# Whole-row loads and another release for the first store in a rotary-embedding kernel

## The chip, the cores and the metric

The kernel runs on one core of one Trainium2 chip. The metric is the device time of one execution in microseconds (us), lower is better. The profile is one execution recorded by the hardware profiler; its span is the time between the first and the last recorded event, a little less than the execution's own time.

## The reference

Rotary position embedding with interleaved pairs. `x` has the shape (8, 2048, 16, 64) in float32, `cos` and `sin` have (2048, 32). All inputs are random normal.

```python
x_pairs = x.reshape(batch, seq_len, num_heads, head_dim // 2, 2)
x1 = x_pairs[..., 0]
x2 = x_pairs[..., 1]
cos = cos[None, :, None, :].copy()
sin = sin[None, :, None, :].copy()
out1 = x1 * cos - x2 * sin
out2 = x1 * sin + x2 * cos
out = np.stack([out1, out2], axis=-1).reshape(batch, seq_len, num_heads, head_dim)
```

67.1 MB of float32 come in and as many go out.

## The kernel before

The text calls one batch entry a row: there are eight, and one holds 2048 positions of 1024 values. The positions are spread over the 128 partitions, 16 consecutive ones (K) on each, so a row is 16384 values per partition. In SBUF the rows stand in bfloat16, in one buffer `rows_sb` with five slots (NX); row b stands in slot b modulo 5. A load from GpSimd's DMA queue turns float32 into bfloat16 on the way, and a store turns it back. A row is 8.4 MB in HBM and 4.2 MB in SBUF.

`rotate` (line 65) works on a row in place with three VectorE operations. The first writes row times sine table into the scratch tile `qt` (line 79), the second multiplies the row by the cosine table (line 80), and the third adds `qt` to the row with the neighbours of each pair exchanged (line 85). The sine table holds the sine with alternating sign, and both tables are repeated over the 16 heads by a stride of zero.

Everything is issued in the order written out by hand, and an instruction waits only for what it needs. The dependencies are tracked per region of a tile. GpSimd issues all DMAs but two; the first four sixteenths of row 0 (the tile `st`) come by SyncE's queue in float32 and are turned to bfloat16 by ScalarE (line 99), and the last four sixteenths of row 7 leave the same way at the end (lines 131 and 132). In GpSimd's order:

- the rest of row 0, `cos`, `sin`, then rows 1 and 2 as one DMA (line 56), row 3 (line 54), and row 4 in two DMAs, its first fourteen sixteenths and then its last two (REST);
- the store of rows 0 and 1 as one DMA (line 63), then the store of row 2 (line 61);
- the load of rows 5 and 6 as one DMA into slots 0 and 1, once those have been stored, and the load of row 7 into slot 2, once that has been stored;
- the store of rows 3 and 4, that of rows 5 and 6, and that of the first twelve sixteenths of row 7.

VectorE builds the tables from `sin` and `cos` (lines 101 to 103), rotates row 0 in two pieces and then the rows 1 to 7.

The store of rows 0 and 1 is held back on purpose by two tiny copies on ScalarE:

```python
nc.scalar.copy(out=mark, in_=rows_sb[:1, 4, K - REST - 1, :1])
nc.scalar.copy(out=rows_sb[:1, 0, 0, :1], in_=rows_sb[:1, 0, 0, :1])
store(0, 2)
```

The first reads one value of row 4 that arrives with its first DMA, the second copies a value of row 0 onto itself. ScalarE goes in order, so the second copy comes after the first, and the store, which reads row 0, comes after both. Near the end, line 130 holds the tail back in the same manner: it writes a value into slot 1 and so waits until row 6 has been stored.

Of the kernel before, what the change touches and what calls it, by code (L numbers as in the profile page):

```python
# [2 lines left out]

# [4 lines left out]


@with_exitstack  # L10
def kernel(
    ctx: ExitStack,
    tc: tile.TileContext,
    x: bass.AP,
    cos: bass.AP,
    sin: bass.AP,
    out: bass.AP,
):
    nc = tc.nc
    fp32 = mybir.dt.float32  # L20
    bf16 = mybir.dt.bfloat16
    mult = mybir.AluOpType.mult
    add = mybir.AluOpType.add

    B, S, H, D = x.shape
    P = 128
    K = S // P
    D2 = D // 2
    HD = H * D
    NX = 5  # L30
    HEAD = 4
    TAIL = 4
    REST = 2

    x_t = x.rearrange("b (p k) h d -> p b k (h d)", p=P, k=K)
    out_t = out.rearrange("b (p k) h d -> p b k (h d)", p=P, k=K)
    cos_t = cos.rearrange("(p k) c -> p (k c)", p=P, k=K)
    sin_t = sin.rearrange("(p k) c -> p (k c)", p=P, k=K)

    consts = ctx.enter_context(tc.tile_pool(name="consts", bufs=1))  # L40
    stage = ctx.enter_context(tc.tile_pool(name="stage", bufs=1))

    cos_sb = consts.tile([P, K * D2], fp32)
    sin_sb = consts.tile([P, K * D2], fp32)
    c_tab = consts.tile([P, K, D], bf16)
    s_tab = consts.tile([P, K, D], bf16)
    mark = consts.tile([1, 1], bf16)

    rows_sb = consts.tile([P, NX, K, HD], bf16)

    def load(b, n=1, k0=0, k1=K):
        s = b % NX
        if n == 1:
            nc.gpsimd.dma_start(out=rows_sb[:, s, k0:k1], in_=x_t[:, b, k0:k1])  # L54
        else:
            nc.gpsimd.dma_start(out=rows_sb[:, s : s + n], in_=x_t[:, b : b + n])  # L56

    def store(b, n=1, k1=K):
        s = b % NX
        if n == 1:  # L60
            nc.gpsimd.dma_start(out=out_t[:, b, :k1], in_=rows_sb[:, s, :k1])  # L61
        else:
            nc.gpsimd.dma_start(out=out_t[:, b : b + n], in_=rows_sb[:, s : s + n])  # L63

    def rotate(b, k0=0, k1=K):

        nk = k1 - k0
        xp = rows_sb[:, b % NX, k0:k1]
        qt = stage.tile([P, K, HD], bf16, name="qt", tag="work")

        def rows(a):
            return a.rearrange("p k (h e) -> p k h e", h=H, e=D)

        def tab(a):
            return dataclasses.replace(
                a, offset=a.offset + k0 * D, ap=[a.ap[0], [D, nk], [0, H], [1, D]]
            )

        nc.vector.tensor_tensor(out=rows(qt[:, :nk]), in0=rows(xp), in1=tab(s_tab), op=mult)  # L79
        nc.vector.tensor_tensor(out=rows(xp), in0=rows(xp), in1=tab(c_tab), op=mult)  # L80
        q_swap = dataclasses.replace(
            qt, offset=qt.offset + 1, ap=[qt.ap[0], [2, nk * HD // 2], [-1, 2]]
        )
        x3 = xp.rearrange("p k (a j) -> p (k a) j", j=2)
        nc.vector.tensor_tensor(out=x3, in0=x3, in1=q_swap, op=add)  # L85
        return qt

    with tc.manual_schedule():
        head = stage.tile([P, HEAD, HD], fp32, name="st", tag="work")
        nc.sync.dma_start(out=head, in_=x_t[:, 0, :HEAD])  # L90
        load(0, k0=HEAD)
        nc.gpsimd.dma_start(out=cos_sb, in_=cos_t)  # L92
        nc.gpsimd.dma_start(out=sin_sb, in_=sin_t)  # L93
        load(1, 2)
        load(3)
        load(4, k1=K - REST)
        load(4, k0=K - REST)

        nc.scalar.copy(out=rows_sb[:, 0, :HEAD], in_=head)  # L99
        s2 = s_tab.rearrange("p k (i j) -> p (k i) j", j=2)  # L100
        nc.vector.tensor_copy(out=s2[:, :, 0], in_=sin_sb)  # L101
        nc.vector.tensor_scalar_mul(s2[:, :, 1], sin_sb, -1.0)  # L102
        nc.vector.tensor_copy(  # L103
            out=c_tab.rearrange("p k (i j) -> p (k i) j", j=2),
            in_=cos_sb.to_broadcast([P, K * D2, 2]),
        )
        rotate(0, 0, HEAD)
        rotate(0, HEAD, K)
        rotate(1)

        nc.scalar.copy(out=mark, in_=rows_sb[:1, 4, K - REST - 1, :1])  # L111
        nc.scalar.copy(out=rows_sb[:1, 0, 0, :1], in_=rows_sb[:1, 0, 0, :1])  # L112
        store(0, 2)
        rotate(2)
        store(2)
        load(5, 2)
        load(7)
        rotate(3)
        rotate(4)
        store(3, 2)  # L120
        rotate(5)
        rotate(6)
        store(5, 2)
        rotate(7)
        store(7, k1=K - TAIL)


        tail = stage.tile([P, TAIL, HD], fp32, name="st", tag="work")
        last = rows_sb[:, 7 % NX]
        nc.scalar.copy(out=rows_sb[:1, 6 % NX, 0, :1], in_=last[:1, K - 1, :1])  # L130
        nc.scalar.copy(out=tail, in_=last[:, K - TAIL :])  # L131
        nc.sync.dma_start(out=out_t[:, B - 1, K - TAIL :], in_=tail)


# [1 line left out]
_INS = ['x', 'cos', 'sin']  # L136
_OUTS = [((8, 2048, 16, 64), 'float32')]


# [23 lines left out]
```

## Time and profile before

| | before |
|---|---|
| time, median of 3 runs | 316.4 us (316.12 to 316.79) |
| the profiled execution's own time | 316.12 us |
| its span | 314.4 us |
| busy VectorE (DVE) | 210.3 us, 67% of the span |
| busy ScalarE (ACT), GpSimd (POOL) | 8.9 us each |
| read from HBM, written to HBM | 67.63 MB, 67.11 MB |
| one VectorE operation on a whole row | 8.69 us |
| VectorE idle ahead of line 79, waiting for loads | 41.2 us, two times |

In the profile, L79 is line 79 of the kernel; an arrow `out<-in` names the tile that is written and the tiles that are read. The names POOLq and SPq stand for the instruction streams of GpSimd and SyncE that issue DMAs, and the DMA share is the mean busy share of the core's 16 DMA engines. It counts packets by the stretch in which they start, so it can be above 1 in a short one. The GB/s count the bytes at the destination: a load counts its bfloat16 bytes, a store its float32 bytes. "To landing" is the time from the issue of a DMA until all of it has arrived.

### The profile page before, as it was taken

What the parts mean: (1) busy time and instruction counts of PE and PEld (TensorE: products, weight loads), DVE (VectorE), ACT (ScalarE), POOL (GpSimd) and SP (SyncE); (2) the same over time, 40 slices, a digit from 0 to 9 for tenths busy, and PEclk for the clock granted to TensorE, in tenths of its full rate; (3) what the DMA queues carried; (4) which work ended last, traced back from release to release, by engine and by line L of the source; (5) the groups of instructions that cost most, each with busy time, mean ns of one, the idle gap of its engine ahead of it and who ended that gap; (6) DMA issues with size and microseconds to landing.
All of it is one profiled execution on the core that took longest, in us unless ns stands there. A gap on an engine that the chain in (4) does not pass through costs nothing.

```text
span 314.4 us, 118 instructions
## 1 busy us (share of the span) xinstructions
DVE 210.3 (67%) x30; ACT 8.9 (3%) x6; POOL 8.9 (3%) x18
## 2 busy tenths in 40 slices
DVE  0009995099999999999992000899999999910000
ACT  1030000000000000000000000000000000000400
POOL 5000000000000000000000000000000000000000
DMA  8999999999999999999999999999999999999997
GB/s 257 260 284 200 200 204 263 200 200 217 225 233 259 400 534 400 400 434 500 400 200 225 242 200 200 229 238 334 400 484 450 400 400 525 409 400 400 434 434 334
DMA packets 2816, 102.24 MB, mean 325 GB/s; under 512 B 256, under 2 KB 256, under 8 KB 512
## 3 DMA queue, kind: packets, MB, share of 16 engines
q0 software_dynamic: 2528, 98.04, 96.8%
q1 hardware_dynamic: 288, 4.19, 3.4%
HBM read 67.63 MB, written 67.11 MB: 429 GB/s over the span
## 4 chain that ended last, share of the span: by engine, by line
DVE 42%; issue 17%; DMA 14%; another core or an unknown queue 13%; ACTq 1%; POOL 0%; ACT 0%; DVEq 0%; POOLq 0%
DMA out_dram<-rows_sb 14%; DVE rows_sb L80 14%; DVE rows_sb L85 14%; DVE qt L79 14%; ACTq L158 1%; POOL out_dram L63 0%; DVE c_tab L103 0%; ACT rows_sb L130 0%; ACTq L130 0%; DVEq L80 0%; DVEq L79 0%; POOLq L63 0%; POOLq L61 0%
## 5 line engine op out<-in xcount | busy, mean ns | idle before, releaser
L79 DVE TENSOR_TENSOR qt<-rows_sb,s_tab 128x16384 bf16<-128x16384 bf16 (+2 forms) x9 | 69.7, 7743 | 41.4 <-DMA rows_sb<-in_x_dram 41.2
L80 DVE TENSOR_TENSOR rows_sb<-rows_sb,c_tab 128x16384 bf16<-128x16384 bf16 (+2 forms) x9 | 69.7, 7743 | 0.4
L85 DVE TENSOR_TENSOR rows_sb<-rows_sb,qt 128x16384 bf16<-128x16384 bf16 (+2 forms) x9 | 69.7, 7744 | 0.3
L101 DVE CAST s_tab<-sin_sb 128x512 bf16<-128x512 f32 x1 | 0.5, 453 | 23.8 <-DMA sin_sb<-in_sin_dram 23.8
L63 POOL DMA_DIRECT2D out_dram<-rows_sb x3 | 2.2, 720 | 183.5 <-ACT rows_sb L112 93.7
L130 ACT COPY rows_sb<-rows_sb 1x1 bf16<-1x1 bf16 x1 | 0.2, 193 | 195.4 <-DMA out_dram<-rows_sb 195.4
L99 ACT CAST rows_sb<-st 128x4096 bf16<-128x4096 f32 x1 | 3.6, 3604 | 13.2 <-DMA st<-in_x_dram 13.2
L131 ACT CAST st<-rows_sb 128x4096 f32<-128x4096 bf16 x1 | 3.6, 3598 | 0.0
L54 POOL DMA_DIRECT2D rows_sb<-in_x_dram x5 | 2.9, 604 | 19.1 <-DMA out_dram<-rows_sb 18.3
L111 ACT COPY mark<-rows_sb 1x1 bf16<-1x1 bf16 x1 | 0.2, 194 | 79.7 <-DMA rows_sb<-in_x_dram 79.7
L61 POOL DMA_DIRECT2D out_dram<-rows_sb x2 | 1.1, 557 | 40.6 <-DVE rows_sb L85 40.6
L56 POOL DMA_DIRECT2D rows_sb<-in_x_dram x2 | 1.5, 728 | 24.7 <-DMA out_dram<-rows_sb 24.7
L99 ACT ACT_TABLE_LOAD x1 | 1.3, 1283 | 0.7 <-PEq L147 0.7
L103 DVE CAST c_tab<-cos_sb 128x1024 bf16<-128x1024 f32 x1 | 0.7, 685 | 0.0
L93 POOL DMA_DIRECT2D sin_sb<-in_sin_dram x1 | 0.6, 564 | 0.0
L92 POOL DMA_DIRECT2D cos_sb<-in_cos_dram x1 | 0.6, 557 | 0.0
L102 DVE TENSOR_SCALAR s_tab<-sin_sb 128x512 bf16<-128x512 f32 x1 | 0.4, 444 | 0.0
L112 ACT COPY rows_sb<-rows_sb 1x1 bf16<-1x1 bf16 x1 | 0.2, 188 | 0.0
L147 POOL MEMSET const-float32-0.0<- 128x1 f32 x1 | 0.1, 99 | 0.2 <-issue 0.2
L147 POOL MEMSET const-bfloat16-1.0<- 128x1 bf16 x1 | 0.1, 102 | 0.0
L147 POOL MEMSET const-float32-1.0<- 128x1 f32 x1 | 0.1, 99 | 0.0
L147 POOL MEMSET const-uint8-127<- 128x1 uint8 x1 | 0.1, 99 | 0.0
## 6 DMA issues: line engine op xcount, KB each, us to landing
rows_sb<-in_x_dram POOLq DMA_DIRECT2D x2, 8192.0 KB, 58.3
rows_sb<-in_x_dram POOLq DMA_DIRECT2D x2, 4096.0 KB, 67.8
out_dram<-rows_sb POOLq DMA_DIRECT2D x1, 6144.0 KB, 34.0
rows_sb<-in_x_dram POOLq DMA_DIRECT2D x1, 3584.0 KB, 94.3
rows_sb<-in_x_dram POOLq DMA_DIRECT2D x1, 3072.0 KB, 21.2
st<-in_x_dram SPq DMA_DIRECT2D x1, 2048.0 KB, 14.4
out_dram<-st SPq DMA_DIRECT2D x1, 2048.0 KB, 15.5
rows_sb<-in_x_dram POOLq DMA_DIRECT2D x1, 512.0 KB, 96.2
```

What stands on the lines that cost most here:

```text
L54: nc.gpsimd.dma_start(out=rows_sb[:, s, k0:k1], in_=x_t[:, b, k0:k1])
L56: nc.gpsimd.dma_start(out=rows_sb[:, s : s + n], in_=x_t[:, b : b + n])
L61: nc.gpsimd.dma_start(out=out_t[:, b, :k1], in_=rows_sb[:, s, :k1])
L63: nc.gpsimd.dma_start(out=out_t[:, b : b + n], in_=rows_sb[:, s : s + n])
L79: nc.vector.tensor_tensor(out=rows(qt[:, :nk]), in0=rows(xp), in1=tab(s_tab), op=mult)
L80: nc.vector.tensor_tensor(out=rows(xp), in0=rows(xp), in1=tab(c_tab), op=mult)
L85: nc.vector.tensor_tensor(out=x3, in0=x3, in1=q_swap, op=add)
L92: nc.gpsimd.dma_start(out=cos_sb, in_=cos_t)
L99: nc.scalar.copy(out=rows_sb[:, 0, :HEAD], in_=head)
L103: nc.vector.tensor_copy(out=c_tab.rearrange("p k (i j) -> p (k i) j", j=2), in_=cos_sb.to_broadcast([P, K * D2, 2]),)
L131: nc.scalar.copy(out=tail, in_=last[:, K - TAIL :])
L158: with _tile.TileContext(nc) as tc:
```

## The change

Each of the rows 1 to 7 is loaded by one DMA of its own: the loads of rows 1 and 2 and of rows 5 and 6 are split by row, and the two parts of row 4 are joined. The two copies on ScalarE that hold back the store of rows 0 and 1 move into the rotation of row 2: the first of them now reads a value of row 2 after VectorE has multiplied that row by the cosine table, and before it adds. The store stands behind the whole `rotate(2)` in the program, and still depends only on rows 0 and 1 and on ScalarE's copy. `rotate` no longer returns `qt`, which no caller used.

```diff
-    REST = 2
...
-    def load(b, n=1, k0=0, k1=K):
-        s = b % NX
-        if n == 1:
-            nc.gpsimd.dma_start(out=rows_sb[:, s, k0:k1], in_=x_t[:, b, k0:k1])
-        else:
-            nc.gpsimd.dma_start(out=rows_sb[:, s : s + n], in_=x_t[:, b : b + n])
+    def load(b, k0=0, k1=K):
+        nc.gpsimd.dma_start(out=rows_sb[:, b % NX, k0:k1], in_=x_t[:, b, k0:k1])
...
-    def rotate(b, k0=0, k1=K):
+    def rotate(b, k0=0, k1=K, between=None):
...
         nc.vector.tensor_tensor(out=rows(xp), in0=rows(xp), in1=tab(c_tab), op=mult)
+        if between is not None:
+            between(xp)
...
-        load(1, 2)
+        load(1)
+        load(2)
         load(3)
-        load(4, k1=K - REST)
-        load(4, k0=K - REST)
+        load(4)
...
-        nc.scalar.copy(out=mark, in_=rows_sb[:1, 4, K - REST - 1, :1])
-        nc.scalar.copy(out=rows_sb[:1, 0, 0, :1], in_=rows_sb[:1, 0, 0, :1])
+        def pass_on(xp):
+            nc.scalar.copy(out=mark, in_=xp[:1, 0, :1])
+            nc.scalar.copy(out=rows_sb[:1, 0, 0, :1], in_=rows_sb[:1, 0, 0, :1])
+
+        rotate(2, between=pass_on)
         store(0, 2)
-        rotate(2)
         store(2)
-        load(5, 2)
+        load(5)
+        load(6)
         load(7)
```

More of the change, by code (lines that the diff above doesn't have):

```diff
@@ L85, in rotate @@
         nc.vector.tensor_tensor(out=x3, in0=x3, in1=q_swap, op=add)
-        return qt
     with tc.manual_schedule():
```

## The prediction

> **What bounds the kernel now.** I read the page first, for who is busy:
>
> ```profile
> span 314.4 us, 118 instructions
> DVE 210.3 (67%) x30; ACT 8.9 (3%) x6; POOL 8.9 (3%) x18
> ...
> DMA  8999999999999999999999999999999999999997
> ...
> q0 software_dynamic: 2528, 98.04, 96.8%
> ```
>
> VectorE works two thirds of the span. The DMA row is full in every one of the 40 slices but the first and the last, and GpSimd's queue alone takes 96.8% of the 16 engines' time. So I asked next whether that row hides holes, with the windows view cut where transfers land (stretch, length, VectorE, ScalarE and GpSimd busy, clock, DMA share, GB/s):
>
> ```profile
> 62.30:81.60 19.30, 19.12 (x3) 0.00 (x0) 0.00 (x0) 1.00 0.99 214
> 81.60:101.00 19.40, 19.33 (x3) 0.29 (x2) 0.72 (x1) 1.00 1.03 247
> 101.00:139.70 38.70, 38.56 (x5) 0.00 (x0) 0.57 (x1) 1.00 1.01 434
> 139.70:159.00 19.30, 19.13 (x4) 0.00 (x0) 0.71 (x1) 1.00 1.02 407
> 159.00:197.60 38.60, 8.15 (x1) 0.00 (x0) 1.28 (x2) 1.00 1.01 217
> ```
>
> Shares of 0.99 to 1.03: nothing idles, whether rows come in (about 200 GB/s of bfloat16, so about 400 read) or go out (about 430), and whether VectorE works (38.56 of 38.70) or waits (8.15 of 38.60). The DMA view of short windows gives each issue's time to landing; with the issue times of the timeline that is when each transfer ends:
>
> ```profile
> rows_sb<-in_x_dram POOLq DMA_DIRECT2D x1, 8192.0 KB, 59.3
> rows_sb<-in_x_dram POOLq DMA_DIRECT2D x1, 4096.0 KB, 77.9
> ...
> rows_sb<-in_x_dram POOLq DMA_DIRECT2D x1, 512.0 KB, 96.2
> ```
>
> Rows 1 and 2, one DMA issued at 3.01, land at 62.3; row 3, issued at 3.71, at 81.6; the last part of row 4, issued at about 4.8, at 101.0. By the same addition the store of rows 0 and 1 (99.12 + 40.5) ends at 139.6, row 2's (115.03 + 43.9) at 158.9, the load of rows 5 and 6 (140.25 + 57.3) at 197.5, row 7's (159.24 + 57.7) at 216.9, the stores of rows 3 and 4 at 255.6 and of 5 and 6 at 294.2, the tail (297.97 + 15.5) at 313.5. Each row costs 19.3 us in either direction, alone or in a pair, and each transfer ends its own length after the one ahead of it, however early it was issued: rows 3 and 4 were queued at 167.45 with loads until 216.9 in front, and did not pass them. One queue, first in first out, never empty from about 2 to 313.5 us. That bounds the kernel. The chain that ended last runs through VectorE for 42% of the span, yet VectorE has gaps of 10.65 and 30.5 us before rows 1 and 5 that move no landing.
>
> The last view is the timeline at the one place where the queue is nearly empty, the first store:
>
> ```profile
> 88.59 8.69 DVE L79 TENSOR_TENSOR qt<-rows_sb,s_tab 128x16384 bf16<-128x16384 bf16 x1
> 97.31 8.69 DVE L80 TENSOR_TENSOR rows_sb<-rows_sb,c_tab 128x16384 bf16<-128x16384 bf16 x1
> 98.54 0.19 ACT L111 COPY mark<-rows_sb 1x1 bf16<-1x1 bf16 x1 [79.74 <-DMA rows_sb<-in_x_dram]
> 98.64 0.19 ACT L112 COPY rows_sb<-rows_sb 1x1 bf16<-1x1 bf16 x1
> 99.12 0.72 POOL L63 DMA_DIRECT2D out_dram<-rows_sb  x1 [93.75 <-ACT rows_sb L112]
> ```
>
> And the DMA view of 98.4 to 102.4, its GB/s in slices of 0.1 us:
>
> ```profile
> GB/s 369 205 82 369 205 82 287 287 82 287 287 82 246 328 82 246 328 82 246 123 4588 1966 3932 0 0 0 0 0 0 0 0 0 0 0 0 0 0 0 0 0
> ```
>
> Small packets of row 4's last part run until the 65 KB store packets start at 100.4 (a packet counts where it starts). From issue to first packet is at most 1.3 us, and the store arrived with only about that to spare.
>
> **The change part by part.**
>
> *Two pair loads become four single ones (rows 1, 2 and 5, 6).* A pair's issue holds GpSimd for 0.71 to 0.74 us, a single's for 0.56 to 0.68, so two more issues are about 2 x 0.4 = 0.8 us of GpSimd. Around 3 us the load of row 0 covers it (it lands at 22.4); at 140 the store of row 2 does, with 19 us to run. Without that cover it would cost the 0.8 whole. On the DMA engines: a pair is 38.6, a single 19.3 to 19.4, so 0, and at most 0.1 a row.
>
> *Row 4 becomes one DMA.* In two parts it took 101.0 - 81.6 = 19.4 against row 3's 19.3: -0.1 us, on the path. An extra completion for the split pairs is inside the rounding. The bounds of these two parts together are -0.3 and +0.3 us; I take -0.1, from the row nearest to it.
>
> *VectorE starts row 1 earlier.* Row 1 alone lands 19.3 before the pair, at 43.0, and row 0's last operation ends at 51.76. So row 1 follows at once, 10.6 us earlier than 62.41. Full operations follow each other at 8.73: row 2 starts at 51.8 + 3 x 8.73 = 78.0, and its cosine product ends at 78.0 + 2 x 8.72 = 95.4 instead of 106.0.
>
> *The release.* From the start of ScalarE's first copy to GpSimd's issue was 99.12 - 98.54 = 0.58, and some 0.1 for the signal from VectorE: issue at about 96.1, 3 us earlier than now. The first packet could go at 97.4; the loads end at 100.9 and the first engine runs dry at 100.3. Spare time grows from none to about 3 us, the queue stays full, and since it is in order an earlier store passes nothing: 0 us. The new wait: VectorE's add of row 2 overwrites what ScalarE reads, so it stands behind the first copy, at most 0.6 us. Behind it are rows 3 and 4, done at 95.4 + 0.6 + 8.7 + 52.4 = 157.1, against 167.15 now. Their store cannot be issued before row 7's load (about 159, behind the landing of row 2's store) and runs from 216.9: 60 us of cover. On GpSimd the store of row 2 and the later loads queue behind the release; row 2's store comes at 104.8 where now it comes at 115.03, 35 us before it is its turn.
>
> *The second half.* The first pair's store ends at about 139.5 as before, loads 5 and 6 go out then, row 5 lands at 178.3 instead of with row 6 at 197.5. VectorE does row 5 from 178.3 to 204.5, row 6 to 230.7, row 7 (landed 216.8) to 256.9. The store of rows 5 and 6 is issued at 231 (now 250.30) and must be there at 255.5; row 7's at 257 (now 276.48), needed at 294.1. Later the tail waits, as now, for the store of 5 and 6 to end. No landing moves.
>
> Sum: 0 + 0 - 0.1 + 0. The profiled execution took 316.12 for its span of 314.4, and becomes 316.0; it is the fastest of three whose median is 316.4, which becomes 316.3. I say 316.2 us.
>
> The Trainium skill (DMA: Bandwidth & Descriptors, "Anatomy of one DMA") gives every DMA on this path about 2.0 us fixed beside its bytes; with one DMA more in all (two splits, one merge) the sum by it would be +2.0, an estimate from that page, 318.2. The landings 19.3 apart do not show it, because the transfers overlap. It is the page beside the first rival.
>
> **The rivals.**
>
> *Each DMA has a price of its own (slower).* If the queue drained between DMAs, the one net addition would pay the latency seen at the first store, 1.3 us: 316.2 + 1.3 = 317.5. Against it: pairs at 38.6 and singles at 19.3 leave no room. It decides if singles land over 0.3 us later than a half pair. 6%.
>
> *The store's descriptors are held up by VectorE (slower).* The issue now falls at the start of row 2's add (95.9 to 104.6). If GpSimd could write nothing to the queue until that ends, the first packet would come at 104.6 + 1.3 = 105.9 and the queue be dry for 5.6 us: 321.8. Against it: at 99.12 the issue fell inside a product that ran to 106.0, and its packets moved at 100.4; row 7's load was issued inside an add in 0.56 us. It decides when no descriptor stands by 100.3. 4%. The Trainium skill (SBUF — State Buffer, "Summary: rules for kernel authors") warns of just this starvation beside VectorE's faster modes, while its section "Who interferes with whom" excludes two-tensor operations; the trace agrees with the exclusion for the product (packets at 100.4), and no row here tests it for the add.
>
> *The change doesn't do what it says (slower).* If row 1 still waited for both loads, VectorE would keep its times, the cosine product would end at 106.0, the store go at 106.7 and its packets at 108: 7.1 us after 100.9, 323.3. For: all rows share one buffer. Against: the two parts of row 4 were told apart (ScalarE went at 98.54, while the last part landed at 101.0). It decides if the release comes after 99.5. 4%.
>
> *The engines do idle before the first store (faster).* Windows of 2 us show shares of 0.67 at 94 to 96 and 0.45 at 96 to 98. Taken as holes they are (0.33 + 0.55) x 2 = 1.8 us, and row 4 as one DMA with a store waiting behind it could return them: 314.4. Against: 1.42 stands at 100 to 102, and the whole of 92 to 106 has 1.02; packets count where they start. 5%.
>
> **How the numbers follow.** 0.2% is 0.63 us, about the spread of the three runs (316.12 to 316.79), and about what a measurement of this kernel can tell from no change. The forecast (-0.1, bounds -0.3 and +0.3) lies inside it, with 75%. Slower: 6 + 4 + 4, and 4 for a wait that I don't see, 18%. Faster: 5 and 2, 7%. The range takes in the forecast with the runs' spread and reaches to the first rival: 315.5 to 317.8; outside are the fast rival, the two of 5 us and more, and part of the unseen, about 17%.
>
> **What would show it right or wrong.** Right: VectorE has no gap before row 1 and about 21 us instead of 30.5 before row 5; the first store is issued at about 96.1; row 1 lands at 43, row 4 at 100.9, the first store at 139.5, the tail at 313.4; every DMA slice but the ends stays full. Wrong: a DMA share well under 1 over the stretch from 95 to 110; a store issued after 99.5; single loads over 19.5 apart; the copies of ScalarE beginning after 96; or a last landing that moves by more than 0.6 us with no hole in the queue, which would mean that packets themselves changed length.

## The result and the profile after

The changed kernel takes 317.32 us (median of 9 runs, 317.15 to 317.51) against 316.4 before; the ratio is 1.0027, 95% interval 1.0018 to 1.0036. It is slower by 0.9 us: the interval leaves out 1, though its lower end lies at about the 0.2% that the prediction counts as no change. The 316.4 is here the median of nine runs of the kernel before (316.12 to 317.17); beside the experiments below, where it ran 16 to 27 times, its median was 316.24 to 316.32. All ratios are against the kernel before. The profiled execution took 317.17 us for a span of 315.4, where the kernel before had 316.12 and 314.4.

The page of the changed kernel, for who is busy:

```profile
span 315.4 us, 120 instructions
DVE 210.4 (67%) x30; ACT 8.9 (3%) x6; POOL 9.0 (3%) x19
...
DMA  7999999999999999999999999999999999999997
...
q0 software_dynamic: 2416, 98.04, 96.7%
```

Nothing seems to have changed: but for its first slice the DMA row is as full as before, with the same 98.04 MB. The microsecond is not a hole. The timeline at the first store has the events where they were forecast (95.4, 96.1, and an add that waits for ScalarE's first copy):

```profile
86.75 8.69 DVE L75 TENSOR_TENSOR rows_sb<-rows_sb,c_tab 128x16384 bf16<-128x16384 bf16 x1
95.48 0.19 ACT L108 COPY mark<-rows_sb 1x1 bf16<-1x1 bf16 x1 [76.64 <-DVE rows_sb L75]
95.58 0.19 ACT L109 COPY rows_sb<-rows_sb 1x1 bf16<-1x1 bf16 x1
95.70 8.69 DVE L82 TENSOR_TENSOR rows_sb<-rows_sb,qt 128x16384 bf16<-128x16384 bf16 x1 [0.26 <-ACT mark L108]
96.06 0.72 POOL L58 DMA_DIRECT2D out_dram<-rows_sb  x1 [90.89 <-ACT rows_sb L109]
```

The DMA view of short windows, around the issue of row 4's load (at 4.58) and that of the first store, gives the landings:

```profile
rows_sb<-in_x_dram POOLq DMA_DIRECT2D x1, 4096.0 KB, 97.5
...
out_dram<-rows_sb POOLq DMA_DIRECT2D x1, 44.6
```

Row 4 lands at 4.58 + 97.5 = 102.1, where the kernel before had it at 101.0; the first store ends at 96.06 + 44.6 = 140.7 instead of 139.6. By the landings in the trace, rows 1 to 3 take 19.23, 19.30 and 19.34 us and row 4 takes 20.37. All later transfers keep their lengths (38.65 for the first store, 38.6 to 38.7 for the later pairs), and the tail lands at 314.5 instead of 313.5. So the whole loss lies in row 4's load. The windows view, cut where the packets start, shows where in it. A row's load is eight waves, each of one packet on each of the 16 engines:

```profile
95.50:97.90 2.40, 2.20 (x1) 0.26 (x2) 0.72 (x1) 1.00 1.01 218
97.90:101.00 3.10, 3.10 (x1) 0.00 (x0) 0.00 (x0) 1.00 1.05 169
101.00:103.40 2.40, 2.40 (x1) 0.00 (x0) 0.00 (x0) 1.00 1.02 437
```

One wave of packets lasts 2.4 us, at 218 GB/s. The last one before the store (the one of 97.9) lasts 3.1 us, at 169 GB/s and with a DMA share of 1.05: the engines are busy all the while, and the same bytes take 0.7 us longer as cut here. By the packet records its 16 packets took 2.9 to 3.6 us, where the other 880 of that size (32 KB) took 2.43 to 2.46. No other queue can be in their way: from 15 to 290 us every packet of this trace is of GpSimd's queue. The turn from row 7's load to the store of rows 3 and 4 has no such wave, though that store was issued at 160.82:

```profile
214.50:216.95 2.45, 2.45 (x1) 0.00 (x0) 0.00 (x0) 1.00 0.99 214
216.95:219.35 2.40, 2.40 (x1) 0.00 (x0) 0.00 (x0) 1.00 1.02 437
```

### The profile page after: what moved, and what is told of

The parts are those of the page before. It is cut to its first block, busy times and chain, and to the rows that moved or that the text cites. A ratio compares the mean times of both kernels' runs of the same rounds, so it can differ in the third digit from the quotient of the medians.

```text
span 315.4 us, 120 instructions
## 1 busy us (share of the span) xinstructions
DVE 210.4 (67%) x30; ACT 8.9 (3%) x6; POOL 9.0 (3%) x19
## 3 DMA queue, kind: packets, MB, share of 16 engines
q0 software_dynamic: 2416, 98.04, 96.7%
## 4 chain that ended last, share of the span: by engine, by line
another core or an unknown queue 63%; DVE 22%; ACTq 1%; ACT 0%; issue 0%
DVE rows_sb L75 8%; DVE qt L74 8%; DVE rows_sb L82 6%; ACTq L157 1%; DVE c_tab L99 0%; ACT rows_sb L129 0%; ACT mark L108 0%; ACT rows_sb L109 0%; ACTq L129 0%
## 5 line engine op out<-in xcount | busy, mean ns | idle before, releaser
L74 DVE TENSOR_TENSOR qt<-rows_sb,s_tab 128x16384 bf16<-128x16384 bf16 (+2 forms) x9 | 69.7, 7743 | 22.8 <-DMA rows_sb<-in_x_dram 22.6
```

## The experiments

Row times below are differences of landings in the trace; "turn" is the place in GpSimd's queue where loads end and a store begins. How far ahead of its turn a store was issued is called its lead; for the first turn it is counted from 100.4, where the store's packets start when nothing is slowed down. Each theory is defined in the expectation that names it first.

**How early the store stands in the queue, and how row 4 is loaded.**

`e1_release_early`: no hold.

```diff
-        rotate(2, between=pass_on)
         store(0, 2)
+        rotate(2)
```

> The changed kernel without the two copies of ScalarE that hold the first store back: the store of rows 0 and 1 is issued right after row 1 is done, at about 78, 23 us ahead of its turn. In the changed kernel the eighth and last packets of row 4's load start 98.0 and last until 101.1 instead of 100.5, so row 4 takes 20.4 us. Theory A (a store that arrives within a few us of its turn disturbs the last load packets in front of it): with 23 us of lead the disturbance has no packet at the end to hit; row 4 takes 19.3, time 316.2 to 316.4, 0.3% faster than the changed kernel. Theory B (the first turn from reading to writing costs 1 us behind full-size packets, whatever the lead): row 4 still takes 20.4, time 317.3.

Store issued at 78.64. Row 4 takes 20.50 us; 317.33, ratio 1.0034 (1.0022 to 1.0047). Theory A falls.

`e2_release_sine`: `between(qt)` called ahead of the cosine product.

> The changed kernel with the release one VectorE operation earlier, behind the sine product of row 2: store issued at about 87.3, 13 us ahead of its turn. Theory A (short lead): row 4 takes 19.3 us, time 316.2 to 316.4; if the disturbance hits whatever runs some 2 us after the issue, a longer wave of packets shows near 89 and the time stays 317.3. Theory B (first turn): the last wave of row 4 is long again, 317.3.

Store issued at 87.52. Row 4 takes 20.23 us, the long wave is again the one of 98; ratio 1.0032 (1.0020 to 1.0045). The long packets belong to the turn and not to the time of the issue: issued at 78.64, 87.52 or 96.06, the store makes the same wave long.

`e3_parts_new_release`:

```diff
-        load(4)
+        load(4, k1=K - 2)
+        load(4, k0=K - 2)
```

> The changed kernel with row 4 loaded in two parts as before (14 and 2 sixteenths), release unchanged at 96.1. Theory A (short lead): the store still arrives 5 us ahead of its turn; if the disturbance takes the packets that run about 2 us after the issue, the last wave of the large part or the small packets are longer and the time is about 317.3. Theory B (first turn, behind full-size packets only): small packets stand ahead of the store, row 4 takes 19.4, time 316.4.

Row 4 takes 20.35 us; ratio 1.0034 (1.0021 to 1.0046). Small packets do not protect, so theory B, which wanted full-size packets, falls. They show better than large ones where the time goes, in the DMA view of 97 to 103, GB/s in slices of 0.15 us:

```profile
GB/s 0 0 0 0 0 0 0 0 82 164 137 137 164 82 109 27 246 109 55 137 191 137 246 191 246 164 273 137 300 546 3550 2185 874 0 0 0 0 0 0 0
```

From 98.2 to 99.85 (eleven slices) the small packets move 119 GB/s on the mean, from there to 101.35 (ten slices) 202. The engines slow down about 3 us ahead of the store's packets and are back at speed before those start.

`e4_singles_old_release`: the kernel before, with only the pair loads split (the cut is against the kernel before).

```diff
-        load(1, 2)
+        load(1)
+        load(2)
...
-        load(5, 2)
+        load(5)
+        load(6)
```

> The kernel before with only the pair loads split (rows 1, 2, 5 and 6 each by its own DMA); row 4 in two parts and the release by its first part stay. Theories A and B agree: 316.4 as before, since the loss lies in row 4's last packets. Rival C (each DMA more has its own price, here two more): 316.9 to 317.3.

316.36 us, ratio 1.0002 (0.9994 to 1.0011). Two more DMAs cost nothing that can be seen: rival C (the first rival of the prediction) falls, and what is left of the change is row 4 in one DMA and the release. With the early release, row 4 in two parts pays as well (e3); with a late one, row 4 in one DMA pays nothing (e6 and e8 below). So it is the release. The small packets that took 3.3 us in the kernel above take 2.5 here (windows view of this kernel):

```profile
98.10:100.60 2.50, 2.50 (x1) 0.28 (x2) 0.72 (x1) 1.00 1.05 210
```

**Where the limit lies, with row 4 in one DMA.** ScalarE's second copy is made longer, n values of row 0 onto themselves on 128 partitions:

```diff
-            nc.scalar.copy(out=rows_sb[:1, 0, 0, :1], in_=rows_sb[:1, 0, 0, :1])
+            row0 = rows_sb[:, 0].rearrange("p k e -> p (k e)")[:, :n]
+            nc.scalar.copy(out=row0, in_=row0)
```

`e6_late_99`, n = 3456:

> The changed kernel, row 4 still one DMA, with ScalarE's second copy made 3456 values on 128 partitions instead of one (a copy of row 0 onto itself, about 3.0 us), so that the store is issued at about 99.1 as before the change. Theory E with the time of arrival deciding (free when the store's descriptors come less than some 2 us before its turn): row 4 takes 19.3, time 316.3. If instead the small packets of row 4's second part were what made the old release free: row 4 takes 20.4, 317.3. Also possible: the store comes too late by a few tenths, 316.3 to 316.8.

`e8_late_984`, n = 2688:

> The same with 2688 values (about 2.4 us): store issued at about 98.5, first packets possible at 99.8. Theory E with arrival deciding: 316.3 to 316.8, between the 97.8 and the 99.1 releases. Theory D: 317.3.

`e7_late_978`, n = 1920:

> The same with 1920 values (about 1.7 us): store issued at about 97.8, first packets possible at 99.1, row 4's loads end at 100.5. Theory E: a part of the cost, 316.5 to 317.3, if the long stretch from 98.3 to 100 is started by the store's arrival; the whole of it, 317.3, if any arrival ahead of the turn pays all. Theory D: 317.3.

| store issued at | row 4 takes | ratio (95%) |
|---|---|---|
| 98.96 (e6) | 19.39 us | 0.9997 (0.9988 to 1.0005) |
| 98.47 (e8) | 19.35 | 0.9997 (0.9988 to 1.0006) |
| 97.67 (e7) | 19.66 | 0.9998 (0.9988 to 1.0007) |
| 96.06 (changed) | 20.37 | 1.0027 (1.0018 to 1.0036) |
| 87.52 (e2) | 20.23 | 1.0032 (1.0020 to 1.0045) |
| 78.64 (e1) | 20.50 | 1.0034 (1.0022 to 1.0047) |

The wave of 97.9 in e6 has its length back, and the store begins at 100.4 (windows view):

```profile
97.90:100.30 2.40, 2.40 (x1) 0.77 (x1) 0.72 (x1) 1.00 1.01 218
100.30:102.70 2.40, 2.40 (x1) 0.00 (x0) 0.00 (x0) 1.00 1.02 437
```

A release 1.9 us ahead of the turn is free. One 2.7 us ahead costs row 4 0.3 us in its profile, where the packets of the last wave took 2.43 to 2.68 us, and nothing that its ten runs show (316.26, where theory E expected 316.5 or more). One 4.3 us ahead or more costs the whole, 0.9 to 1.2 us of row 4's time. So the time of arrival decides, as theory E had it; why the second turn is free it does not say. All of the change but its release, with a later release, is as fast as the kernel before and not measurably faster.

**Which store pays.** The second turn, at 218, paid nothing in any of the runs so far, with a store 57 us ahead of it. Eight kernels ask what tells the first from the second.

`e5_small_write_first`:

```diff
+    first = consts.tile([P, 256], fp32)
...
+        nc.scalar.copy(out=first, in_=rows_sb[:, 0, 0, :256])
+        nc.sync.dma_start(out=out_t[:, 0, 0, :256], in_=first)
         rotate(0, HEAD, K)
```

> The changed kernel plus one small extra write: after the first piece of row 0, ScalarE copies 256 values per partition to a float32 tile and SyncE's queue writes them to their place in the output, at about 33 (the store of rows 0 and 1 writes the same values again). It moves 0.13 MB, about 0.3 us of the DMA engines. Theory D (the cost belongs to the first write to HBM of each engine, wherever it stands): the long packets move to about 33 to 36 and row 4's load takes 19.3 us instead of 20.4; the time stays near 317.3 to 317.6, or falls to 316.6 if the small write pays nothing. Theory E (the cost belongs to a store standing in GpSimd's queue behind loads at the turn): row 4 still takes 20.4, time 317.5.

The small write goes out from 37.4 on, no 32 KB packet near it is long, and row 4 takes 20.26 us; 1.0035 (1.0021 to 1.0049). Theory D falls, as far as a small write by the other queue can show it.

`e9_two_single_stores`: `store(0)` and `store(1)` for `store(0, 2)`.

> The changed kernel with its first store as two DMAs of one row each, released at 96.1 as there. Known so far: the store standing in the queue by about 98 makes row 4's last packets long; released at 98.5 or later it doesn't; and the second turn from loads to a store (row 7 to rows 3 and 4, near 218) pays nothing though that store stands 57 us ahead. Theory I (the shape of the two-row store is part of it): row 4's load takes 19.3 us. Theories F, G, H (first store of GpSimd's queue; slots; place in the queue's ring): it takes 20.2 to 20.5, time 317.3.

Row 4 takes 20.55 us; 1.0032 (1.0017 to 1.0047). The store's shape is not it (theory I).

`e10_other_slots`: `(b + 3) % NX` for `b % NX`.

> The changed kernel with row b in slot (b+3) modulo 5, so that at the first turn the store reads slots 3 and 4 while the load fills slot 2, just as at the second turn of the changed kernel. Theory G (which slots are read and written at the turn decides): row 4's load takes 19.3 us, and the second turn may pay instead. Theories F, H: row 4's load takes 20.2 to 20.5, time 317.3.

Row 4 takes 20.32 us and the second turn's load 19.31; 1.0032 (1.0020 to 1.0044). Nor are the slots (theory G).

`e12_more_loads`: rows 1 to 3 in four DMAs each.

> The changed kernel with each of the rows 1, 2 and 3 loaded in four DMAs instead of one (nine more DMAs ahead of the first store), release at 96.1 as there. Theory H (the cost belongs to a certain place in the ring of descriptors, in which the first store stands by chance): row 4's load takes 19.3, or the long packets move. Theory F: row 4 takes 20.2 to 20.5. The split loads may cost up to 0.1 us each beside that (row 4 in two parts cost 0.1).

Row 4 takes 19.99 us, the long packets stay in its last wave; 1.0030 (1.0015 to 1.0045). Nor is the place in the queue (theory H). Row 3 lands at 82.28 instead of 81.68, so the nine loads more cost at most 0.07 us each.

`e11_small_store_in_front`:

```diff
         load(3)
-        load(4)
...
         rotate(0, 0, HEAD)
+        nc.gpsimd.dma_start(out=out_t[:, 0, 0, :256], in_=rows_sb[:, 0, 0, :256])
+        load(4)
```

> The changed kernel plus one small store on GpSimd's own queue (256 bfloat16 values per partition of row 0, turned to float32, written again by the large store) between the loads of rows 3 and 4, issued at about 32. Theory F (the first store of GpSimd's queue pays, whichever it is): the load of row 3 takes about 20.3 instead of 19.3 and that of row 4 takes 19.3. Theory H (the place of the large store in the queue, or its own first use): row 4's load takes 20.2 to 20.5 still. The time is 317.3 plus 0.1 to 0.3 for the extra bytes in both cases.

Row 3 takes 19.36 us, the small store 0.35, row 4 20.07; 1.0026 (1.0016 to 1.0036). A small store in the same queue neither pays nor spares the large one, so theory F falls.

`e13_second_store_late`: the store of rows 3 and 4 held until row 5 is done.

```diff
-        store(3, 2)
         rotate(5)
+        nc.scalar.copy(out=mark, in_=rows_sb[:1, 5 % NX, 0, :1])
+        nc.scalar.copy(out=rows_sb[:1, 3, 0, :1], in_=rows_sb[:1, 3, 0, :1])
+        store(3, 2)
```

> The changed kernel with the store of rows 3 and 4 held back, by two such copies of ScalarE, until row 5 is done (about 205.5), 12 us ahead of its turn at 218 instead of 57. Theory L (a store pays when it joins the queue while few loads are left in front, some 5 to 23 us): row 7's load takes 20.3 us instead of 19.3, and the time is 318.3. Theory M (the first long store of a run pays, later turns don't): row 7 takes 19.3, time 317.3.

That store is issued at 206.28. Row 7's load, issued at 160.38, lands at 218.1, after 19.31 us of its own, as in the changed kernel; 1.0027 (1.0016 to 1.0038). Its line in the DMA view, and the last wave ahead of that store in the windows view:

```profile
rows_sb<-in_x_dram POOLq DMA_DIRECT2D x1, 4096.0 KB, 57.7
...
214.80:217.20 2.40, 2.40 (x1) 0.00 (x0) 0.00 (x0) 1.00 1.01 218
```

`e14_first_store_very_early`: no hold, `store(0)` behind `rotate(0, HEAD, K)` and `store(1)` behind `rotate(1)`.

> The changed kernel without the hold, with rows 0 and 1 stored by one DMA each as soon as they are done: store of row 0 issued at about 52, 49 us ahead of its turn, with nearly three loads in front. Theory L: row 4's load takes 19.3 us, time 316.3. Theory M: it takes 20.2 to 20.5, time 317.3.

Store issued at 52.43, 48 us ahead. Row 4 takes 20.51 us; 1.0031 (1.0020 to 1.0043). Theory L falls with these two runs.

`e15_store_between_loads`: e14 (its removal of the hold is not shown again), with row 4's load behind the first store.

```diff
-        load(4)
...
+        store(0)
+        load(4)
         rotate(1)
+        store(1)
```

> As e14, with the load of row 4 behind the store of row 0 in GpSimd's queue: the first turn from a load to a store comes at the end of row 3's load (near 82), the second at the end of row 4's (near 121). Theory M: row 3's load takes 20.3 us and row 4's 19.3. Theory L (30 us of lead at the first of these turns, 42 at the second): both take 19.3, time 316.3. A turn from a store to a load has cost nothing so far; if more turns cost something by themselves, the time is above 317.3.

The long packets move with the turn (windows view; loads at about 200 GB/s, stores at 437), and the wave ahead of the second turn, the last line, is not long:

```profile
76.30:78.60 2.30, 2.27 (x2) 0.00 (x0) 0.27 (x1) 1.00 0.95 199
78.60:81.80 3.20, 3.20 (x1) 0.00 (x0) 0.27 (x1) 1.00 0.99 154
81.80:84.20 2.40, 2.40 (x1) 0.00 (x0) 0.00 (x0) 1.00 1.02 437
...
118.00:120.40 2.40, 2.40 (x1) 0.00 (x0) 0.00 (x0) 1.00 1.01 218
```

Row 3 takes 20.50 us, row 4, at the second turn, 19.30. More turns cost nothing: 317.39, 1.0034 (1.0021 to 1.0047). Theory M fits every run whose first whole-row store was issued 4.3 us or more ahead of its turn. That store costs 0.7 to 1.2 us, once, taken from the load in front of it; the turns behind it are free. The packet records say the same. In the eleven of these kernels that load row 4 in one DMA, exactly 16 packets of 32 KB took longer than 2.6 us, those of the wave ahead of the first whole-row store; in the kernel before, in e4, e6 and e8 none did.

What the engines do in these 1.6 us stays open. The slow stretch comes too soon to be the store's own packets by their recorded start, and a store of 256 values per partition does not set it off; which size does was not tried. Something that is fetched or set up once for a long store, or a buffer that such a store fills ahead of its turn and that later never empties, are guesses that no run tests.

## Why the prediction was wrong

**The step that failed** is the release: "Spare time grows from none to about 3 us, the queue stays full, and since it is in order an earlier store passes nothing: 0 us." The queue did stay full, and nothing was passed. But a full queue is not a queue at speed. The term is +1.1 us: row 4 took 20.37 where 19.3 was forecast. With that term the sum is 316.0 + 1.1 = 317.1, against 317.17 measured for the profiled execution. The last of the prediction's signs of being wrong is what came: the last landing moved by 1.0 us, from 313.5 to 314.5, with no hole in the queue, because packets had changed length. It stood there as a sign only; no rival and no term of the sum had a price for it.

**The evidence that misled** was the store of rows 3 and 4, which stands in front of the second turn for 50 us and costs nothing. It was read as a rule for all turns. e13 and e14 show that the first long store differs from the later ones, with leads of 12 us for the second and 48 us for the first. The profile of before cannot show it, as its first store comes 1.3 us ahead of its turn, and there the cost is nothing (e6, e8). The late release that looked as if it had no time to spare was the feature that saved the microsecond.

**What held.** Row 1 follows row 0 without a gap (51.85), the store was issued at 96.06 (forecast 96.1), the later stores at 231.97 and 258.15 (231 and 257), VectorE's idle time before row 5 fell to 22.6 us (21), and single loads take 19.2 to 19.4 us. The -0.1 for row 4 in one DMA is within the noise: 19.35 and 19.39 in e8 and e6 against 19.42 before.

**The rivals.** A price for each DMA is excluded by e4: two more DMAs, 1.0002 with an upper end of 1.0011, at most 0.17 us each. The Trainium skill (DMA: Bandwidth & Descriptors, "Anatomy of one DMA") would have given 2.0 us for each if they added up; in this queue, which is never empty, they did not. Descriptors held up by VectorE: the store was issued inside the add that ran from 95.70 to 104.4, and its packets started at 101.1, so the add does not hold them until it ends. In e6 the store was issued at 98.96, inside the same add, and its packets started at 100.4, 1.4 us later, against 1.3 in the kernel before. The Trainium skill (SBUF — State Buffer, "Who interferes with whom") reports that `tensor_tensor` did not stall such a DMA; the trace now agrees for the add as for the product. The separate wait for row 1 did what it says. The windows of 2 us with low shares were no holes: in e6, with row 4 in one DMA, the store's packets start at 100.4 as in the kernel before. None of the four named rivals was the cause. It lay in the 4% for something unseen, and that the measured time is inside the range is luck: only the first rival, a wrong one, had stretched it so far.

## What to carry to other kernels

When a kernel is bound by a DMA queue, compare the length of each transfer by its landings, not only the busy share: packets that take longer leave the share at 1, as the 1.05 of the long wave shows. A cost that one place of the trace does not show is not excluded at another; a first use can differ from a second. Before a hold on a DMA is moved to release it earlier, measure a kernel that changes the release alone. Here every release tried 4.3 us or more ahead of the queue running dry cost about 1 us, whether 4 us or 48 us ahead, and those 1.3 to 1.9 us ahead cost nothing.

## What the runs showed of the hardware that was not expected

The first whole-row store in GpSimd's queue slows the loads in front of it for about 1.6 us, to 119 GB/s where 202 follow (e3), if it was issued 4.3 us or more ahead of its turn: 20.0 to 20.6 us for a row instead of 19.3, in twelve kernels. Issued 2.7 us ahead it costs a row 0.3 us (e7); issued 1.9 us ahead or less, nothing that shows (before, e4, e6, e8). Later whole-row stores cost nothing with 12 us (e13), 42 us (the second store of e15, issued at 78.33) or 57 us of lead. Why the first one differs is not known.
